# HGRN2 scores of 16 keys and fewer as 32 x 32 strips, sums with ones on four strips, mLSTM products on array halves

## The chip, the cores and the metric

The kernel runs on one core of one Trainium2 chip. A core has five engines with a queue of their own each: TensorE (PE, its weight loads are PEld), VectorE (DVE), ScalarE (ACT), GpSimd (POOL) and SyncE (SP), which here only starts DMAs. They share SBUF and PSUM, both of 128 partitions, and wait for each other through semaphores. The metric is the time of one execution in microseconds. Before the change it was 952.54 us, the median of three runs (952.47 to 953.07).

## What is computed

One decoder layer over 512 tokens of width 1024, in float32: a half-step SwiGLU feed-forward, a token mixer, and a second half-step feed-forward, each between RMS norms. The change is in the mixer, which projects the normalised tokens once and runs two recurrences on the columns, four heads of HGRN2 and four of mLSTM:

```python
def hgrn2(q, k, v, log_f):          # k = 1 - f, 4 heads, dk = dv = 128
    # S_t = diag(f_t) S_{t-1} + k_t v_t^T,  o_t = S_t^T q_t, by chunks:
    G = cumsum(log_f)
    o_inter = (q * exp(G)) @ S
    scores[t, s] = sum_d q[t, d] * k[s, d] * exp(G[t, d] - G[s, d])   # s <= t
    o = o_inter + scores @ v
    S = exp(G_end) * S + (k * exp(G_end - G)).T @ v

def mlstm(q, k, v, log_i, log_f):   # 4 heads, dqk = 64, dv = 128
    # m_t is the running maximum that keeps the exponents small
    P = (q @ k.T) * exp(D - m_t)
    num = inter * (q @ C) + P @ v;   den = inter * (q @ n) + sum(P)
    h = num / max(abs(den), exp(-m_t))
    C = keep * C + (w * k).T @ v;    n = keep * n + (w * k).sum()
```

Before mLSTM, its q and k columns go through a causal depthwise convolution of four taps with a bias, and SiLU. Both outputs are normalised, gated and projected back.

## The kernel before

Tokens stand in four chunks of 128 (`NT`), and both recurrences are worked by chunks of 128. The large matrix products are made of fp32r parts: every weight tile is split into a high and a low part (`split`: a cast on ScalarE, L208, a subtraction on VectorE, L210), and each product is three matmuls (`mm3`, L126 to L128, with 512 moving columns; `in_k`, L433, with 256). Small products are plain fp32: a matmul then appears in the trace as two instructions.

The mixer (`mixer`, L1371) runs a chain of small work on all engines, and fills TensorE's time between its steps with the projections. These stand in `self.jobs` as generators: `fill(n)` takes n steps of the next jobs, a step being three matmuls of 512 columns or six of 256; `until(name)` takes steps until a job is done. So the order on TensorE is written out by hand, as far as the program goes; a scheduler then orders each engine's queue by what is ready, keeping the dependences. `FILL` (L27) says how many steps are taken between two levels of head pair 0, of pair 1, between the mLSTM value stages and between the HGRN2 value stages.

HGRN2's scores with their decay inside the sum are made level by level for a pair of heads (`hgrn_levels`, L1065). At level c (64, 32, 16, 8, 4, 2) each block of 2c tokens has c keys and the c queries behind them; both are scaled by the decay to the block's middle (`hgrn_level`, L1032): VectorE makes two differences (L1044 for qe, L1045 for el), ScalarE their exponents (L1046, and L1047 into `ke`), VectorE multiplies by q (L1049). Then come eight chunk-and-head products (L1057). At 64 and 32, keys of the block stand as 64 or 32 stationary columns and write to the partitions of those keys. Below 32 all 128 keys of a chunk are multiplied with all 64 queries of that level, and VectorE picks the wanted entries by a mask (`put`, L1030, a copy with a predicate into `sT`, keys on partitions, 16 chunk-and-head blocks of 128 queries). At 64 and 32 ScalarE copies the block (L1027). Two `ke` tiles take turns.

The diagonal and the neighbours (level 1, `hgrn_lowest`, L984) are sums over the 128 features: VectorE makes "one" = q·k (L994) and "near" (L996, L997), both are split in high and low parts (ScalarE L995 and L998 into tiles that carry the tags of the norm gains, gpre and gpost; VectorE L1000, L1001), and TensorE multiplies them by a 128 x 128 matrix of ones (L1007), which puts the sum on all partitions; VectorE takes the diagonal by the mask `eye` (L1012). The tile "one" and the later "ek" (`hgrn_decays`, L969 and L970), whose transposes (L981) give the keys for the state, share one buffer of the tag xn.

The convolution (`conv`, L1188) copies the projection from PSUM (ScalarE, L1192) and makes four products on VectorE, the first with the bias (L1195), three added to it (L1198). In mLSTM, `mlstm_scores` makes the state products of three chunks for both head pairs (L1287): keys of two heads on 128 columns with the values of both heads, 258 columns, of which only the two diagonal blocks are kept. `mlstm_values` (L1324) multiplies the queries of a pair with the state C (L1332, 258 columns, zero off the diagonal blocks) and adds the scores times the values (L1335); then ScalarE squares, VectorE and GpSimd make the factor and VectorE scales.

`masks` (L883) makes ones, masks and eye on GpSimd. Scratch tiles of 512 columns come from a ring of four buffers (`st`), PSUM tiles from a ring of eight banks (`ps`).

Of the kernel before, what the change touches and what calls it, by code (L numbers as in the profile page):

```python
# [14 lines left out]
P = 128  # L15
# [11 lines left out]
FILL = (6, 5, 2, 2)  # L27
NH = 4
W = 512
# [38 lines left out]
class Layer:  # L68
# [814 lines left out]
    def masks(self, mc, mb):  # L883

        nc = self.nc

        self.ones = mb.tile([P, P], F32R, name="ones")
        nc.gpsimd.tensor_copy(self.ones, self.one.broadcast_to([P, P]))
        self.mask = mb.tile([P, len(LEVELS), 64], I32, name="mask")
        nc.gpsimd.memset(self.mask, 1)  # L890
        for n, c in enumerate(LEVELS):
            m = self.mask[:, n, :].rearrange("p (b c) -> p b c", c=c)
# [4 lines left out]
        self.eye = mb.tile([P, P], I32, name="eye")  # L897
        nc.gpsimd.memset(self.eye, 1)
        nc.gpsimd.affine_select(
            self.eye, self.eye, pattern=[[1, P]], compare_op=ALU.is_equal, fill=0.0, base=0, channel_multiplier=-1  # L900
        )

        sel = mb.tile([4, 6, 2, 64], F32, tag="tmp", bufs=1, name="sel")
        nc.gpsimd.memset(sel, 1.0)
# [79 lines left out]
    def hgrn_lowest(self, p):  # L984

        nc = self.nc
        q, kk = self.q[p], self.kk[p]
        flat = lambda t: t.rearrange("p a t -> p (a t)")
        by2 = lambda t: flat(t).rearrange("p (b two) -> p b two", two=2)
        by_a = lambda t: t.rearrange("p (a t) -> p a t", a=2)  # L990
        hi, lo = (by_a(self.cp.tile([P, D], F32R, tag=tag, bufs=1, name=self.nm(tag))) for tag in ("gpre", "gpost"))
# [3 lines left out]
        nc.scalar.copy(hi, one)  # L995
# [4 lines left out]
        nc.vector.tensor_tensor(lo, one, hi.bitcast(F32), op=ALU.subtract)  # L1000
        nc.vector.tensor_tensor(nlo, near, nhi.bitcast(F32), op=ALU.subtract)  # L1001
        yield
        scs = []
        for ops in ((hi[:, 0], lo[:, 0]), (hi[:, 1], lo[:, 1]), (nhi, nlo)):
            sc = self.ps()
            for n, m in enumerate(ops):
                nc.tensor.matmul(sc, self.ones, m, start=n == 0, stop=n == 1)  # L1007
            scs.append(sc)
        yield
        for a in range(2):  # L1010
            h = 2 * p + a
            nc.vector.copy_predicated(  # L1012
                self.sT[:, 4 * h : 4 * h + 4, :], self.eye[:, None, :].broadcast_to([P, NT, P]),
                scs[a].rearrange("p (n s) -> p n s", s=P),
            )
        self.put(p, 0, scs[2])
        yield

    def put(self, p, n, sc):

        c = LEVELS[n]
        so = self.sT[:, 8 * p : 8 * p + 8, :].rearrange("p n (b two c) -> p n b two c", two=2, c=c)[:, :, :, 1, :]
        if c >= 32:
# [5 lines left out]
        mk = self.mask[:, n : n + 1, :].broadcast_to([P, 8, 64]).rearrange("p n (b c) -> p n b c", c=c)  # L1029
        self.nc.vector.copy_predicated(so, mk, sc.rearrange("p (n b c) -> p n b c", n=8, c=c))  # L1030

    def hgrn_level(self, p, n, ke):  # L1032
# [19 lines left out]
        k8, q8 = flat(ke).rearrange("p (n s) -> p n s", s=P), qe.rearrange("p (n u) -> p n u", u=64)  # L1052
        for m in range(8):
            for b in range(1 if c < 32 else 64 // c):
                r = slice(2 * c * b, 2 * c * b + c) if c >= 32 else slice(0, P)
                u = slice(c * b, c * b + c) if c >= 32 else slice(0, 64)
                nc.tensor.matmul(  # L1057
                    sc[r, 64 * m + u.start : 64 * m + u.stop], k8[:, m, r], q8[:, m, u], start=True, stop=True,
                    skip_group_check=True,
                )  # L1060
# [4 lines left out]
    def hgrn_levels(self, p, kes, per, then=lambda: None):  # L1065
# [3 lines left out]
        next(L[0])  # L1069
# [19 lines left out]
        next(L[N - 1])  # L1089

# [97 lines left out]
    def conv(self, n, ps):  # L1188
# [6 lines left out]
        nc.vector.tensor_scalar(y, x, tap(3), self.prm[:, 16 + n : 17 + n], op0=ALU.mult, op1=ALU.add)  # L1195
# [33 lines left out]
    def mlstm_scores(self, mc):  # L1229
# [54 lines left out]
        for c in range(3):  # L1284
            for p in range(2):
                ps = self.ps()
                nc.tensor.matmul(  # L1287
                    ps[:, :258], self.kw[:, p, c, :], self.vm[:, c, 2 * p : 2 * p + 2, :].rearrange("p a v -> p (a v)"),
                    start=True, stop=True,
                )  # L1290
# [33 lines left out]
    def mlstm_values(self, c):  # L1324
# [3 lines left out]
        pm = []  # L1328
        for p in range(2):
            ps = self.ps()  # L1330
            if c:
                nc.tensor.matmul(ps[:, :258], self.qdm[:, p, (c - 1) * P : c * P], self.C[:, p, c - 1, :], start=True, stop=False)  # L1332
            for a in range(2):
                o = ps[:, 129 * a : 129 * a + 129]
                nc.tensor.matmul(o, self.pT[:, 2 * p + a, s], self.vm[:, c, 2 * p + a, :], start=c == 0, stop=c == 0 or a == 1)  # L1335
            pm.append(ps[:, :258].rearrange("p (a v) -> p a v", a=2))
        sq = self.sp.tile([P, 512], F32, tag="junk", bufs=1, name=self.nm("sq"))
        den, ab, ss, r = self.col(4), self.col(4), self.col(4), self.col(4)
        for p in range(2):
            nc.scalar.activation(sq[:, 256 * p : 256 * p + 256].rearrange("p (a v) -> p a v", a=2), pm[p][:, :, :P], AF.Square)  # L1340
        yield
        for p in range(2):
            nc.vector.tensor_copy(den[:, 2 * p : 2 * p + 2].rearrange("p (a o) -> p a o", o=1), pm[p][:, :, P : P + 1])
# [9 lines left out]
        for p in range(2):  # L1353
            nc.vector.tensor_tensor(
                self.y[:, c, W + 256 * p : W + 256 * p + 256].rearrange("p (a v) -> p a v", a=2),
                pm[p][:, :, :P],
                f[:, 2 * p : 2 * p + 2].rearrange("p (a o) -> p a o", o=1).broadcast_to([P, 2, P]),
# [195 lines left out]
```

## Time and profile before

| | us |
|---|---|
| median of three runs | 952.54 |
| the profiled execution | 953.22 |
| its span, first to last instruction | 951.5 |
| TensorE busy in it | 941.4 |
| VectorE busy | 714.3 |
| ScalarE busy | 466.1 |
| GpSimd busy | 291.2 |

The mixer with its projections lies between about 360 and 600 us of the span. In a row of the profile the first name is the source line and engine, then the operation, the tile written and the tiles read, the shape, and the count; a duration in the timeline is that of the whole group in that row, from the first start to the last end. Matmuls overlap each other, so what one costs is read from start to start, or from the chain of waits, which counts each stretch of time once.

### The profile page before, as it was taken

To read this page: it belongs to the slowest core of one execution; us is meant where nothing else is said; L and a number is where in the kernel's file an instruction comes from. 1 tells how busy PE (TensorE), PEld (TensorE's weight loads), DVE (VectorE), ACT (ScalarE), POOL (GpSimd) and SP (SyncE) were. 2 spreads that over 40 slices of the span, in tenths; PEclk is the share of its full clock that TensorE was granted. 3 is DMA by queue.
4 is the path that set the end of the run, shared out by engine and by line. 5 is a ranking of instruction groups with operands and counts; after the bars stand their busy time and mean duration, and the time that the engine had idled before them with its cause. 6 is when DMAs were issued, how large, how long until landed. Compare 5 with 4: busy or idle time off the path is not lost.

```text
span 951.5 us, 15926 instructions
## 1 busy us (share of the span) xinstructions
PE 941.4 (99%) x6567; PEld 865.2 (91%) x6567; DVE 714.3 (75%) x798; ACT 466.1 (49%) x632; POOL 291.2 (31%) x225
## 2 busy tenths in 40 slices
PE   9999999999999999999999999999999999999997
PEld 7999999999888889998788888999999999988885
DVE  6798999998445376799856555797999999843543
ACT  7645454445344356966523345763445444533431
POOL 3546555751000036200010300354655565100001
PEclk9999999999999999999999999999999999999999
DMA  9243333325322014321312126214334332322202
GB/s 319 81 134 113 110 120 124 113 91 175 110 90 89 1 36 121 90 90 49 129 45 72 42 87 196 90 48 128 102 105 129 116 112 89 109 96 105 89 1 88
DMA packets 81666, 95.97 MB, mean 101 GB/s; under 512 B 4117, under 2 KB 61497, under 8 KB 81594
## 3 DMA queue, kind: packets, MB, share of 16 engines
q1 hardware_dynamic: 81306, 94.44, 31.0%
q8 instruction: 51, 0.84, 0.4%
q10 hardware_dynamic: 288, 0.52, 0.2%
q14 instruction: 21, 0.17, 0.1%
HBM read 92.85 MB, written 2.10 MB: 100 GB/s over the span
## 4 chain that ended last, share of the span: by engine, by line
PE 96%; DVE 2%; issue 1%; ACT 1%; DMA 0%; POOL 0%; DVEq 0%; POOLq 0%; ACTq 0%
PE ps L488 45%; PE ps L126 12%; PE ps L128 12%; PE ps L127 12%; PE ps L433 6%; PE ps L1057 2%; PE ps L267 2%; PE ps L443 1%; PE ps L115 0%; PE ps L1130 0%; PE ps L1335 0%; PE ps L1308 0%; PE ps L1332 0%; PE ps L1097 0%; PE ps L1310 0%
## 5 line engine op out<-in xcount | busy, mean ns | idle before, releaser
L210 DVE TENSOR_TENSOR w<-raw,w 128x1024 fp32r<-128x1024 f32 x214 | 363.0, 1704 | 123.1 <-ACT w L208 122.9
L208 ACT CAST w<-raw 128x1024 fp32r<-128x1024 f32 x214 | 224.0, 1053 | 314.6 <-PE ps L128 114.2
L222 POOL TENSOR_TENSOR raw<-raw,raw 128x1024 f32<-128x1024 f32 x80 | 221.0, 2764 | 170.8 <-DVE w L210 160.3
L488 PE MATMUL ps<-xq,w 128*128 128x256 f32 x2016 | 238.1, 277 | 0.0
L488 PEld LDWEIGHTS ps<-xq,w 128*128 128x128 f32 x2016 | 233.7, 188 | 0.2
L488 PE MATMUL ps<-sq,w 128*128 128x256 f32 x1440 | 171.0, 277 | 0.0
L488 PEld LDWEIGHTS ps<-sq,w 128*128 128x128 f32 x1440 | 167.4, 188 | 0.0
L128 PE MATMUL ps<-w,hs 128*128 128x512 f32 x336 | 131.0, 390 | 0.0
L126 PE MATMUL ps<-w,hs 128*128 128x512 f32 x336 | 130.9, 390 | 0.0
L127 PE MATMUL ps<-w,hs 128*128 128x512 f32 x336 | 130.8, 389 | 0.0
L126 PE MATMUL ps<-w,xq 128*128 128x512 f32 x208 | 84.7, 407 | 0.1
L128 PE MATMUL ps<-w,xq 128*128 128x512 f32 x208 | 81.1, 391 | 0.0
L127 PE MATMUL ps<-w,xq 128*128 128x512 f32 x208 | 81.1, 390 | 0.0
L128 PEld LDWEIGHTS ps<-w,hs 128*128 128x128 f32 x336 | 63.1, 188 | 13.8 <-DVE hs L672 0.7
L127 PEld LDWEIGHTS ps<-w,hs 128*128 128x128 f32 x336 | 63.1, 188 | 12.9
L126 PEld LDWEIGHTS ps<-w,hs 128*128 128x128 f32 x336 | 63.1, 188 | 12.8
L354 POOL TENSOR_SCALAR col<-col 128x1 f32<-128x1 f32 x24 | 9.5, 397 | 203.2 <-ACT junk L353 203.1
L433 PE MATMUL ps<-xq,w 128*128 128x256 f32 x480 | 55.7, 277 | 0.0
L433 PEld LDWEIGHTS ps<-xq,w 128*128 128x128 f32 x480 | 55.1, 188 | 0.1
L672 DVE TENSOR_TENSOR hs<-hf,hs 128x1024 fp32r<-128x1024 f32 x42 | 51.1, 1218 | 0.0
L128 PEld LDWEIGHTS ps<-w,xq 128*128 128x128 f32 x208 | 39.1, 188 | 8.9 <-DVE xq L274 0.3
L126 PEld LDWEIGHTS ps<-w,xq 128*128 128x128 f32 x208 | 39.1, 188 | 8.7 <-ACT xq L273 0.7
(241 smaller groups left out, 963.4 us busy)
## 6 DMA issues: line engine op xcount, KB each, us to landing
raw<-in_ffn_w_in_dram SPq DMA_DIRECT2D x88, 512.0 KB, 4.1
raw<-in_ffn_w_out_dram SPq DMA_DIRECT2D x44, 512.0 KB, 3.4
raw<-in_w_mix_in_dram SPq DMA_DIRECT2D x28, 512.0 KB, 3.7
raw<-in_w_mix_out_dram SPq DMA_DIRECT2D x8, 512.0 KB, 3.5
out_dram<-xs SPq DMA_DIRECT2D x8, 256.0 KB, 2.0
xs<-in_x_dram SPq DMA_DIRECT2D x6, 256.0 KB, 6.8
gpost<-in_norm_post_dram SPq DMA_DIRECT2D x3, 512.0 KB
gpre<-in_norm_pre_dram SPq DMA_DIRECT2D x2, 512.0 KB, 4.1
```

The costliest lines, as they stand in the source:

```text
L126: mm(ps, sh, mh, start=start, stop=False, **kw)
L127: mm(ps, sh, ml, start=False, stop=False, **kw)
L128: mm(ps, sl, mh, start=False, stop=stop, **kw)
L208: nc.scalar.copy(hi, raw)
L210: nc.vector.tensor_tensor(lo, raw, hi.bitcast(F32), op=ALU.subtract)
L222: nc.gpsimd.tensor_tensor(o, o, c, op=ALU.add)
L267: self.nc.tensor.transpose(pt[:, c * P : (c + 1) * P], src[:, k * P : (k + 1) * P], self.ident)
L433: mm(ps[:, u0:u1], w[:, a, k, :], self.xop(k, b, u0, u1), start=k + n + m == 0, stop=k == ND - 1 and n == 2, skip_group_check=True,)
L443: self.nc.tensor.matmul(ps[:, :HALF], w[:, a, k, :], self.xop(k, b, 0, HALF), start=m + k == 0, stop=m == 2 and k == ND - 1)
L488: self.nc.tensor.matmul(ps[:, c], wb[b][:, k, v], left[d][:, k, :], start=first and a + n + k == 0, stop=n == 2 and k == KH - 1, skip_grou ...
L672: self.nc.vector.tensor_tensor(t[:, 1], src, t[:, 0].bitcast(F32), op=ALU.subtract)
L1057: nc.tensor.matmul(sc[r, 64 * m + u.start : 64 * m + u.stop], k8[:, m, r], q8[:, m, u], start=True, stop=True, skip_group_check=True,)
```

## The change

- The levels of 16, 8, 4 and 2 multiply each strip of 32 keys with the 16 queries that its own blocks have (four matmuls per chunk and head, writing to four groups of 32 partitions). VectorE's masked copies go into a new compact tile D (keys on partitions, 32 queries of the same strip); when all levels are made, `spread` copies D's four strips into sT on ScalarE.
- The level of 64 is made in two strips of 32 keys.
- The sums with ones take "one" and "near" as they are, in fp32, without splitting; each strip of 32 partitions sums its own 32 (or 16) columns only.
- mLSTM's state product is made per head on half the columns of the array, the query-times-state product per head on half its rows; the PSUM banks then hold one head of each pair instead of both heads of one pair.
- The first product of the convolution, with the bias, moves from VectorE to ScalarE.
- FILL[0] is 7 instead of 6. The masks are made wide in scratch tiles, and compacted by eight copies on GpSimd.

```diff
-FILL = (6, 5, 2, 2)
+FILL = (7, 5, 2, 2)
...
-        self.ones = mb.tile([P, P], F32R, name="ones")
-        nc.gpsimd.tensor_copy(self.ones, self.one.broadcast_to([P, P]))
-        self.mask = mb.tile([P, len(LEVELS), 64], I32, name="mask")
-        nc.gpsimd.memset(self.mask, 1)
+        self.ones = mb.tile([P, 32], F32, name="ones")
+        nc.gpsimd.memset(self.ones, 1.0)
+        self.D = mb.tile([P, 16, 32], F32, name="D")
+        nc.gpsimd.memset(self.D, 0.0)
...
+        self.mask = mb.tile([P, n16, 16], I32, name="mask")
+        self.eye = mb.tile([P, 32], I32, name="eye")
+        wide = self.st("wide", dt=I32)[:, : 64 * n16].rearrange("p (n c) -> p n c", n=n16)
+        square = self.st("square", P, dt=I32)
...
+        for b in range(4):
+            r = slice(32 * b, 32 * b + 32)
+            nc.gpsimd.tensor_copy(self.mask[r], wide[r, :, 16 * b : 16 * b + 16])
+            nc.gpsimd.tensor_copy(self.eye[r], square[r, r])
...
-        near, nhi, nlo = self.st("near"), self.st("nhi", dt=F32R), self.st("nlo", dt=F32R)
+        near = self.st("near")
         nc.vector.tensor_tensor(one, q, kk, op=ALU.mult)
-        nc.scalar.copy(hi, one)
...
-        nc.scalar.copy(nhi, near)
-        yield
-        nc.vector.tensor_tensor(lo, one, hi.bitcast(F32), op=ALU.subtract)
-        nc.vector.tensor_tensor(nlo, near, nhi.bitcast(F32), op=ALU.subtract)
-        yield
-        scs = []
-        for ops in ((hi[:, 0], lo[:, 0]), (hi[:, 1], lo[:, 1]), (nhi, nlo)):
-            sc = self.ps()
-            for n, m in enumerate(ops):
-                nc.tensor.matmul(sc, self.ones, m, start=n == 0, stop=n == 1)
-            scs.append(sc)
-        yield
-        for a in range(2):
-            h = 2 * p + a
-            nc.vector.copy_predicated(
-                self.sT[:, 4 * h : 4 * h + 4, :], self.eye[:, None, :].broadcast_to([P, NT, P]),
-                scs[a].rearrange("p (n s) -> p n s", s=P),
-            )
-        self.put(p, 0, scs[2])
+        yield
+        sc = self.ps()
+        for v, t, w in ((sc[:, :256], one.rearrange("p a (c t) -> p (a c) t", c=NT), 32), (sc[:, 256:384], near.rearrange("p (n t) -> p n t", n=8), 16)):
+            for b in range(4):
+                nc.tensor.matmul(
+                    v[32 * b : 32 * b + 32].rearrange("p (n t) -> p n t", n=8), self.ones, t[:, :, w * b : w * b + w],
+                    start=True, stop=True, skip_group_check=True,
+                )
+        yield
+        nc.vector.copy_predicated(
+            self.D[:, 8 * p : 8 * p + 8, :], self.eye[:, None, :].broadcast_to([P, 8, 32]), sc[:, :256].rearrange("p (n t) -> p n t", n=8)
+        )
+        self.put(p, 0, sc[:, 256:384])
...
-        if c >= 32:
+        if c > 16:
...
+        so = self.D[:, 8 * p : 8 * p + 8, :].rearrange("p n (b two c) -> p n b two c", two=2, c=c)[:, :, :, 1, :]
+        mk = self.mask[:, n : n + 1, :].broadcast_to([P, 8, 16]).rearrange("p n (b c) -> p n b c", c=c)
+        self.nc.vector.copy_predicated(so, mk, sc[:, :128].rearrange("p (n b c) -> p n b c", n=8, c=c))
+
+    def spread(self, p):
+
+        for b in range(4):
+            r = slice(32 * b, 32 * b + 32)
+            self.nc.scalar.copy(self.sT[r, 8 * p : 8 * p + 8, r], self.D[r, 8 * p : 8 * p + 8, :])
...
+        if c == 64:
+            blocks = [(slice(s, s + 32), slice(0, 64), 0) for s in (0, 32)]
+        elif c == 32:
+            blocks = [(slice(64 * b, 64 * b + 32), slice(32 * b, 32 * b + 32), 32 * b) for b in range(2)]
+        else:
+            blocks = [(slice(32 * b, 32 * b + 32), slice(16 * b, 16 * b + 16), 0) for b in range(4)]
         for m in range(8):
-            for b in range(1 if c < 32 else 64 // c):
...
+            for r, u, o in blocks:
+                o += m * (64 if c > 16 else 16)
+                nc.tensor.matmul(sc[r, o : o + u.stop - u.start], k8[:, m, r], q8[:, m, u], start=True, stop=True, skip_group_check=True)
...
         next(L[N - 1])
+        self.spread(p)
...
-        nc.vector.tensor_scalar(y, x, tap(3), self.prm[:, 16 + n : 17 + n], op0=ALU.mult, op1=ALU.add)
+        nc.scalar.activation(y, ps, AF.Identity, scale=tap(3), bias=self.prm[:, 16 + n : 17 + n])
...
-                nc.tensor.matmul(
-                    ps[:, :258], self.kw[:, p, c, :], self.vm[:, c, 2 * p : 2 * p + 2, :].rearrange("p a v -> p (a v)"),
-                    start=True, stop=True,
-                )
+                for a in range(2):
+                    r, v = slice(64 * a, 64 * a + 64), slice(129 * a, 129 * a + 129)
+                    nc.tensor.matmul(
+                        ps[r, v], self.kw[:, p, c, r], self.vm[:, c, 2 * p + a, :], start=True, stop=True, skip_group_check=True
+                    )
...
-            if c:
-                nc.tensor.matmul(ps[:, :258], self.qdm[:, p, (c - 1) * P : c * P], self.C[:, p, c - 1, :], start=True, stop=False)
...
+        banks = [self.ps() for _ in range(2)]
+        if c:
+            for p in range(2):
+                for a in range(2):
+                    r = slice(64 * a, 64 * a + 64)
+                    nc.tensor.matmul(
+                        banks[a][:, 129 * p : 129 * p + 129], self.qdm[r, p, (c - 1) * P : c * P],
+                        self.C[r, p, c - 1, 129 * a : 129 * a + 129], start=p == 0, stop=False, skip_group_check=True,
+                    )
+        for a in range(2):
+            for p in range(2):
+                o = banks[a][:, 129 * p : 129 * p + 129]
+                nc.tensor.matmul(
+                    o, self.pT[:, 2 * p + a, s], self.vm[:, c, 2 * p + a, :], start=c == 0, stop=True, skip_group_check=True
+                )
```

The lines of the changed kernel stand somewhat further down: its level matmuls are L1068, the transposes of ek L989, the state product L1297, query times state L1342, scores times values L1349; the sums keep L1007.

More of the change, by code (lines that the diff above doesn't have):

```diff
@@ L1021, in put @@
         c = LEVELS[n]
-        so = self.sT[:, 8 * p : 8 * p + 8, :].rearrange("p n (b two c) -> p n b two c", two=2, c=c)[:, :, :, 1, :]
-        if c >= 32:
+        if c > 16:
+            so = self.sT[:, 8 * p : 8 * p + 8, :].rearrange("p n (b two c) -> p n b two c", two=2, c=c)[:, :, :, 1, :]
             sc3 = sc.rearrange("p (n b c) -> p n b c", n=8, c=c)
@@ L1068, in hgrn_levels @@
         N = len(L)
-        next(L[0])
         next(L[0])
@@ L1327, in mlstm_values @@
         s = slice(c * P, (c + 1) * P)
-        pm = []
-        for p in range(2):
-            ps = self.ps()
-            if c:
[L1332 to L1336, printed above, removed]
+        banks = [self.ps() for _ in range(2)]
[13 more added lines that the diff above has]
+                )
+        pm = [ps[:, :258].rearrange("p (q v) -> p q v", q=2) for ps in banks]
+        of = lambda t, a: t.rearrange("p (q a v) -> p a q v", q=2, a=2)[:, a]
         sq = self.sp.tile([P, 512], F32, tag="junk", bufs=1, name=self.nm("sq"))
@@ L1354, in mlstm_values @@
             nc.vector.tensor_tensor(
-                self.y[:, c, W + 256 * p : W + 256 * p + 256].rearrange("p (a v) -> p a v", a=2),
+                of(self.y[:, c, W:], p),
                 pm[p][:, :, :P],
-                f[:, 2 * p : 2 * p + 2].rearrange("p (a o) -> p a o", o=1).broadcast_to([P, 2, P]),
+                of(f, p).broadcast_to([P, 2, P]),
                 op=ALU.mult,
```

23 lines of the change are left out of this document (7 added, 16 removed).

## The prediction

> **What bounds the kernel now.** I read the page first: its shares of busy time, then the chain that ended last.
>
> ```profile
> span 951.5 us, 15926 instructions
> PE 941.4 (99%) x6567; PEld 865.2 (91%) x6567; DVE 714.3 (75%) x798; ACT 466.1 (49%) x632; POOL 291.2 (31%) x225
> PE 96%; DVE 2%; issue 1%; ACT 1%; DMA 0%; POOL 0%; DVEq 0%; POOLq 0%; ACTq 0%
> ```
>
> TensorE is busy 99% of the span and makes 96% of the chain, so a change pays by what it takes from TensorE's own queue or from TensorE's waits; time taken from the other engines pays only where they make TensorE wait. So the second view was what TensorE waits for, and the third the busy times by stage of the mixer.
>
> ```profile
> PE ps L1057 <- ACT ke L1047: 1.5, 1, 1.5
> ```
> ```profile
> 398.00:440.00 42.00, 42.00 (x359) 40.00 (x358) 40.53 (x57) 30.76 (x42) 0.00 (x0) 1.00 0.23 73
> 440.00:460.00 20.00, 18.52 (x92) 15.20 (x92) 18.47 (x24) 12.31 (x16) 0.00 (x0) 1.00 0.33 109
> 460.00:490.00 30.00, 30.00 (x218) 26.11 (x216) 16.73 (x24) 11.84 (x20) 0.93 (x1) 1.00 0.29 86
> 490.00:545.00 55.00, 54.95 (x314) 45.55 (x313) 35.26 (x101) 20.79 (x37) 12.85 (x21) 1.00 0.15 49
> ```
>
> The columns are the stretch, its length, then busy time of PE, PEld, DVE, ACT and POOL, the granted clock, and the DMA. In the whole mixer TensorE stands still once, for 1.5 us before the level of 64 of head pair 1. VectorE is full (40.5 of 42 us) through pair 0 and (18.5 of 20) up to that wait. The clock is 1.00 throughout.
>
> **TensorE's part, term by term.** The chain at two levels of pair 1 shows what blocks of either kind cost (start, us, what):
>
> ```profile
> 465.92 0.63 PE ps L1057 x32
> 466.55 0.43 PE ps L126
> 466.98 0.23 PE ps L127
> ...
> 470.18 1.73 PE ps L1057 x16
> 471.91 0.29 PE ps L126
> ```
>
> The level of 32 already works on strips of 32 keys: 16 matmuls, two passes each, 32 instructions in 0.63 us, 19.7 ns each; the first filler matmul behind it takes 0.43 us against the usual 0.23, so leaving the strips costs 0.20. The level of 16, with all 128 keys as the stationary side, takes 1.73 us for 16 instructions (108 ns each) and 0.06 to leave, 1.79 together.
>
> *Levels of 16, 8, 4, 2* (eight blocks over two pairs): each becomes 32 matmuls of a 32-key strip and 16 queries, 64 instructions. No row shows 16 moving columns. The nearest row is the level of 32, with the same strip and twice the columns: 64 × 19.7 = 1.26, plus 0.20 to leave, 1.46 in place of 1.79, a gain of 0.33 a block and 2.6 in all. If the four strips run side by side where the level of 32 uses two, an instruction costs half, the block 0.83, the gain is 7.7. The other bound is the rival below.
>
> By the Trainium skill, "TensorEngine Tiling (Array Packing)", Key Properties, a change of tiling mode drains the engine; the 0.20 us behind the strips agrees. By "TensorE: Matmul & The Clock Gate", "Wait — 56ns, not 53.3ns?", starts never come closer than about 25 ns however few columns there are; the 19.7 ns here are below that, and the row decides. An estimate by that page would be 64 × 25 = 1.6 us a block, and no gain from the levels.
>
> *Level of 64* (two blocks): now 16 instructions with 64 stationary columns, ending where the transposes begin:
>
> ```profile
> 410.74 1.15 PE L1057 MATMUL ps<-qe,ke 128*64 128x64 f32 x16
> 411.82 0.87 PE L981 MATMUL ps<-ident,ek 128*128 128x128 f32 x6
> ```
>
> 1.08 us from start to start, 67.5 ns each. After: two strips of 32, 32 instructions, 64 moving columns. Bounds 32 × 19.7 = 0.63, and 1.08 if the columns that stream set the time as now and two strips halve it. I take 0.98, nearer the latter since the columns stay: gain 0.2 for both pairs (0 to 0.9). The level of 32 keeps its instructions.
>
> *Sums with ones* (twice): now six fp32r matmuls of 512 columns, in one pass each; after, sixteen instructions in fp32, since every matmul takes two passes: 8 of 256 columns and 8 of 128 on four strips, 3072 columns.
>
> ```profile
> 399.04 0.40 PE L1007 MATMUL ps<-gpre,ones 128*128 128x512 f32 x1
> 400.44 0.63 PE L433 MATMUL ps<-xq,w 128*128 128x256 f32 x4
> ```
> ```profile
> 499.96 1.16 PE L1223 MATMUL ps<-qk 64*128 64x128 f32 x16
> 500.88 0.48 PE L1185 MATMUL ps<-nm,selr 36*128 36x512 f32 x1
> ```
> ```profile
> 527.95 0.60 PE L1332 MATMUL ps<-C,qdm 128*128 128x258 f32 x2
> 528.38 0.61 PE L1335 MATMUL ps<-vm,pT 128*128 128x129 f32 x4
> ```
>
> Now: 400.44 − 399.04 = 1.40. The fp32 column costs 0.43/(2 × 258) = 0.83 ns on the whole array (L1332) and 0.92/(16 × 128) = 0.45 ns where matmuls alternate between two halves (L1223). Four strips in order b = 0 to 3, both passes of one strip following each other, can overlap neighbours as the halves do: 3072 × 0.45 = 1.38, plus 0.20 to leave, 1.58: a loss of 0.18 each, 0.4 together. Bounds: no overlap 2.56 + 0.20, a loss of 2.7 for both; all four at once 0.64 + 0.20, a gain of 1.1. I take the halves, whose order is the same. The bound by strips that never overlap is far from the level of 32, where they do.
>
> *mLSTM states and values.* The state product of a chunk is four instructions of 258 columns now:
>
> ```profile
> 512.31 1.03 PE L1287 MATMUL ps<-vm,kw 128*128 128x258 f32 x4
> 513.00 0.58 PE L126 MATMUL ps<-w,xq 128*128 128x512 f32 x1
> 513.41 0.39 PE L127 MATMUL ps<-w,xq 128*128 128x512 f32 x1
> ```
>
> From start to the second filler 1.10, less one filler of 0.23: 0.87. After: eight of 129 columns on alternating halves, 8 × 129 × 0.45 = 0.46 and 0.20 to leave, 0.66; gain 0.2, three chunks. The query-times-state product (L1332, four of 258 columns over both pairs, 0.86) becomes the same eight on row halves, in three chunks: 0.2 each again. Together 1.2 (bounds: no overlap, 0.86 + 0.20, a loss of 1.2; no cost of leaving, a gain of 2.5). The products with pT keep count and shape.
>
> Sum on TensorE: 2.6 + 0.2 − 0.4 + 1.2 = 3.6.
>
> **The wait of 1.5 us.** It is VectorE's queue, not ScalarE's: just ahead of ke stands el.
>
> ```profile
> 458.43 0.61 DVE el L1045
> ...
> 459.06 0.64 ACT ke L1047
> ...
> 459.78 1.12 PE ps L1057 x16
> ```
> ```profile
> L1030 DVE COPY_PREDICATED sT<-mask,ps 128x512 f32<-128x512 int32 x6 | 6.1, 1021 | 0.1
> L1012 DVE COPY_PREDICATED sT<-eye,ps 128x512 f32<-128x512 int32 x4 | 2.7, 736 | 0.0
> L969 DVE TENSOR_TENSOR ek<-G,kk 128x1024 f32<-128x1024 f32 x2 | 2.5, 1226 | 0.1
> L1000 DVE TENSOR_TENSOR gpost<-one,gpre 128x1024 fp32r<-128x1024 f32 x2 | 2.4, 1223 | 0.8 <-ACT gpre L995 0.8
> L1195 DVE TENSOR_SCALAR qk<-cx,prm 128x512 f32<-128x512 f32 x4 | 2.1, 534 | 0.0
> L1001 DVE TENSOR_TENSOR nlo<-near,nhi 128x512 fp32r<-128x512 f32 x2 | 1.4, 688 | 0.1
> ```
>
> The change takes from VectorE both subtractions (1.2 + 0.7 a pair) and the four conv products (2.1), lets one eye copy of 256 columns replace two of 512, and cuts each masked copy from 512 to 128 columns; at a quarter of its 1.0 us a masked copy keeps some 0.3, an estimate. Between 440 and 459 us alone that is a subtraction, two masked and two eye copies: about 0.7 + 1.5 + 1.1 = 3.3 us, more than the 1.5. In the built program VectorE also makes the level-64 operands of pair 1 ahead of the copies of the sums, and FILL[0] of 7 puts seven more steps of filler (three matmuls of 0.23) before them: 4.8 us more cover. The wait goes: 1.5. What is late next is nothing I can find: for the levels of pair 1 five steps and a block are 5 × 0.69 + 1.46 = 4.9 us each, and VectorE is busy 16.7 of 30 us there even now.
>
> **Costed at nothing.** The seven steps are taken from later filler: the built program still has an unbroken run of filler ahead of the turn of y; without it they would bare the latencies of the value stages. ScalarE loses two casts a pair and gains four conv products and eight copies of D to sT:
>
> ```profile
> L1027 ACT COPY sT<-ps 32x256 f32<-32x256 f32 (+1 forms) x6 | 2.6, 433 | 0.0
> L1409 ACT ACTIVATE q<-ps 128x512 f32<-128x512 f32 x4 | 2.4, 600 | 0.0
> ```
>
> 8 × 0.43 + 4 × 0.60 = 5.9 us, spread over stretches where it is idle 11 of 42, 8 of 20 and 18 of 30 us; sT is read only after mLSTM. A new wait: ek (L969) shares its buffer with "one", which the sums now read, so ek stands behind TensorE's sums, and behind ek in VectorE's queue the sums' copies and the next el. TensorE has 36 fillers (8.3 us) between the sums of pair 1 and the transposes of ek; ek takes 1.2 there and about 1.1 on ScalarE as exponent; without that cover it would cost 2.3. GpSimd makes more masks and copies, which nothing reads before the sums at 399, and then it idles for long:
>
> ```profile
> 386.62 0.73 POOL L904 MEMSET sel<- 4x768 f32 x1 [11.99 <-DVE G L946]
> ```
>
> On SP's queue the loads of gpost and gpre move up (their tiles no longer serve the sums), between the weight loads at 350 to 362 us.
>
> ```profile
> 354.24 0.70 DVE L390 TENSOR_TENSOR ps<-ps,gpost 128x512 f32<-128x512 f32 x1
> 349.81 9.10 SPq L183 DMA_DIRECT2D raw<-in_w_mix_in_dram  x4
> ```
>
> The gpost load waits for the last reader of the old gain, done at 354.9, and the weight load behind it is the third of those four, whose own buffer comes free later; no delay. A late weight would cost its lateness.
>
> **The sum.** 3.6 + 1.5 = 5.1. The profiled execution took 953.22 us (span 951.5 and 1.7 around it), 0.7 above the median of 952.54. So 948.1 on its scale, 947.4 on the median's.
>
> **Rivals.**
> 1. *The issue of small instructions sets the time (slower).* The eight blocks carry 512 instructions. The transposes of 4 × 4 start 60 ns apart:
>
> ```profile
> 461.72 0.20 PE L1174 MATMUL ps<-ident,z 4*128 4x4 f32 x1
> 461.78 0.20 PE L1173 MATMUL ps<-ident,z 4*128 4x4 f32 x1
> ```
>
> At that price the levels lose 512 × 40 = 20.6 us: 968. It decides from 19.7 + 5.1/0.512 = 29.7 ns on. Against it: the level of 32 issues at 19.7, and those transposes all sit on the same array rows.
> 2. *A floor near 25 ns.* At (1.79 − 0.20)/64 = 24.8 ns a block gains nothing: 947.4 + 2.6 = 950.0. This is the case of the rule that the Trainium skill, "TensorE: Matmul & The Clock Gate", gives above.
> 3. *Strips and halves don't overlap in the longer matmuls.* Sums lose 2.7, mLSTM 1.2, the level of 64 gains nothing: 2.6 − 2.7 − 1.2 + 1.5 = 0.2, so 952.3: nothing measurable. For it: passes of one strip follow each other; against it: L1223.
> 4. *Four strips side by side.* Levels 7.7, sums 1.1: with the rest 7.7 + 0.2 + 1.1 + 1.2 + 1.5 = 11.7, so 940.8.
>
> **How the numbers follow.** Forecast 0.56, rival 1 0.11, rival 2 0.12, rival 3 0.11, rival 4 0.10. About 0.2% (1.9 us) is what a measurement here can tell from no change. Faster: 0.56 + 0.10 + most of rival 2, 0.08, is 0.74; same 0.11 + 0.04 = 0.15; slower 0.11. The range holds forecast, rivals 2 and 3 and the nearer half of 4: 942.5 to 952.5; the forecast's own is 944.5 to 950.
>
> **What would show it.** The L1068 blocks of 64 instructions at 1.2 to 1.3 us with 0.4 for the filler behind; L1007 of sixteen instructions at 1.4 to 1.6; L1297 and L1342 at about 0.46 a chunk; no wait of TensorE in the levels; VectorE below 36 of 42 us in pair 0. Wrong if an L1068 block takes over 1.6, or if TensorE waits for ke, ek or a weight.

## The result

The changed kernel takes 943.58 us (median of five runs, 943.38 to 943.65); the kernel before took 952.85 on the same chip (five runs, 952.47 to 953.55). The ratio is 0.9902, 95% interval 0.9889 to 0.9916: 9.3 us are gone where 5.1 were forecast. The measured time lies 3.8 us below the forecast of 947.4: inside the whole range (942.5 to 952.5), outside the forecast's own (944.5 to 950), and a good half of the way towards the rival with four strips side by side (940.8).

The page of the changed kernel, its span, busy times and the chain's shares:

```profile
span 941.9 us, 16851 instructions
...
PE 933.0 (99%) x7027; PEld 851.7 (90%) x7027; DVE 701.1 (74%) x788; ACT 470.0 (50%) x641; POOL 291.1 (31%) x234
...
PE 92%; DVE 3%; POOL 2%; issue 1%; ACT 1%; DVEq 0%; POOLq 0%; ACTq 0%
```

TensorE is busy 8.4 us less, with 460 matmul records more. The chain has passed from TensorE to the others in two places, and 5% of it now lies on VectorE and GpSimd: ahead of the mixer (343 to 360 us), and in the mixer's value stages (513 to 552 us). The waits of TensorE in the mixer after the change (total, times, longest), and three stretches with the columns that the prediction names:

```profile
PE ps L128 <- DVE xq L274: 0.3, 1, 0.3
PE ps L126 <- DVE y L1371: 0.3, 1, 0.3
PE ps L267 <- DVE hf L372: 0.2, 1, 0.2
```
```profile
398.00:440.00 42.00, 42.00 (x541) 38.29 (x540) 36.32 (x51) 35.71 (x48) 0.00 (x0) 1.00 0.29 87
440.00:460.00 20.00, 20.00 (x190) 15.72 (x189) 16.34 (x24) 12.77 (x21) 0.00 (x0) 1.00 0.22 62
...
482.00:537.00 55.00, 54.69 (x334) 43.15 (x334) 36.35 (x102) 20.07 (x37) 10.99 (x19) 1.00 0.18 58
```

The wait of 1.5 us before the level of 64 is gone; three of 0.2 to 0.3 have come, on hf at 360 us, on y at 524 and on xq at 552. VectorE is down to 36.3 of 42 us through pair 0, still a little over the 36 that were forecast. The chain of the changed kernel at the places of the change (start, us, what), and a level of 16 queries or fewer in its timeline:

```profile
411.92 1.02 PE ps L1068 x32
...
418.53 0.63 PE ps L1068 x32
...
436.54 0.67 PE ps L1068 x51
437.21 0.43 PE ps L126
437.64 0.23 PE ps L127
...
449.28 0.79 PE ps L1007 x16
450.06 0.43 PE ps L126
```
```profile
436.47 0.74 PE L1068 MATMUL ps<-qe,ke 128*32 128x16 f32 x64
```

A level of 16 queries takes 0.67 us where 1.73 stood and 1.26 was forecast (the chain counts 51 of the block's 64 instructions; the timeline has all of them). That is 0.67/64, 10.5 ns an instruction. Leaving costs 0.43 − 0.23 = 0.20, as forecast, so a block costs 0.87 in place of 1.79. The sixteen instructions of the sums take 0.79, and 0.20 to leave, where 1.40 stood and 1.58 was forecast. The level of 64 takes 1.02, where 1.08 stood, and the level of 32 (the row of 0.63) is as it was.

To compare kernels without what lies outside the mixer, I take the stretch from the first sums with ones to the first turn of y, in the timeline of the changed kernel and of the one before:

```profile
398.86 0.64 PE L1007 MATMUL ps<-one,ones 128*32 128x256 f32 x8
...
549.56 1.91 PE L267 MATMUL ps<-ident,y 128*128 128x128 f32 x16
```
```profile
559.20 1.91 PE L267 MATMUL ps<-ident,y 128*128 128x128 f32 x16
```

Before: 559.20 − 399.04 = 160.16 us (the first sum stands in the prediction). After: 549.56 − 398.86 = 150.70. The stretch gives 9.46 us, about as much as the whole kernel gives (9.3 by the medians, 951.5 − 941.9 = 9.6 by the spans of these two profiled executions), so the explanation is to be found in it. In each experiment below it is taken from the same two rows.

### The profile page after: what moved, and what is told of

Same layout as the page of the kernel before. It is cut to its first block, busy times and chain, and to the rows that moved or that the text cites. A ratio compares the mean times of both kernels' runs of the same rounds, so it can differ in the third digit from the quotient of the medians.

```text
span 941.9 us, 16851 instructions
## 1 busy us (share of the span) xinstructions
PE 933.0 (99%) x7027; PEld 851.7 (90%) x7027; DVE 701.1 (74%) x788; ACT 470.0 (50%) x641; POOL 291.1 (31%) x234
## 4 chain that ended last, share of the span: by engine, by line
PE 92%; DVE 3%; POOL 2%; issue 1%; ACT 1%; DVEq 0%; POOLq 0%; ACTq 0%
PE ps L488 46%; PE ps L126 12%; PE ps L128 12%; PE ps L127 12%; PE ps L433 6%; PE ps L267 1%; PE ps L1068 1%; POOL col L259 1%; POOL col L354 0%; DVE w L216 0%; PE ps L1138 0%; PE ps L115 0%; PE ps L122 0%; DVE y L1330 0%; ACT junk L353 0%
## 5 line engine op out<-in xcount | busy, mean ns | idle before, releaser
L126 PEld LDWEIGHTS ps<-w,xq 128*128 128x128 f32 x208 | 39.1, 188 | 10.2 <-issue 1.6
```

The source lines that it names most:

```text
L126: mm(ps, sh, mh, start=start, stop=False, **kw)
```

## The experiments

Of the theories, the first says that matmuls on different strips of 32 columns run side by side, and those on the same strip behind one another, so that the order over strips sets the time of a block. The rivals are that each instruction has a price of its own, whatever the order, or that the gain came from elsewhere (VectorE's relief, the filler, mLSTM). Each diff is against the changed kernel unless it says otherwise.

### The order over the strips

The same 64 instructions of a level block, in another order: all eight chunk-and-head blocks of one strip before the next strip, or two strips in turn and then the other two.

```diff
-        for m in range(8):
-            for r, u, o in blocks:
+            seq = [(m, blk_) for blk_ in blocks for m in range(8)]
...
+            for m, (r, u, o) in seq:
```
```diff
...
+            seq = [(m, blk_) for two in (blocks[:2], blocks[2:]) for m in range(8) for blk_ in two]
...
```

> The changed kernel, but in the levels of 16 to 2 the eight matmuls of one strip follow each other before the next strip's (same 64 instructions a block, other order). Strips side by side (a matmul overlaps its neighbour only on another strip): the block rises from 0.67 us to about four times, 64 x 42 ns = 2.7 us, eight blocks +16 us, about 960 us. Issue of small instructions alone (10.5 ns each, whatever the strip): block 0.67 us, 943.6 us.

> The changed kernel, with the strips of the levels of 16 to 2 taken in alternating pairs (strips 0 and 1 for all eight chunks and heads, then 2 and 3). Strips side by side: two overlap, as in the level of 32, 19.7 ns an instruction, block 1.26 us, +0.6 us x 8 = +4.7 us, about 948.3 us. Issue alone: block 0.67 us, 943.6 us.

Strip by strip the kernel took 952.82 us (one run), with a stretch of 159.86; two strips in turn 945.77 (945.71 to 946.61; ratio to before 0.9928, 0.9913 to 0.9943), stretch 153.39. The chain of the two, strip by strip first:

```profile
438.90 1.83 PE ps L1072 x64
440.73 0.43 PE ps L126
```
```profile
442.80 1.03 PE ps L1072 x62
443.82 0.43 PE ps L126
```

The block takes 1.83, 1.03 and 0.67 us with one, two and four strips in turn: 28.6, 16.1 and 10.5 ns an instruction. The exit costs 0.20 each time. Nothing but the order differs, so a price per instruction alone can't be the cause. Both orders cost time, as strips side by side would have it, and both less than was expected (952.82 against 960, 945.77 against 948.3): one strip in a row costs 2.7 times the four in turn, and not four times. Eight blocks of 1.83 − 0.67 make 9.3 us, and the stretch is 9.2 longer than that of the changed kernel, so the gain is gone: 952.82 us stand against 952.89 for the kernel before in the same set. With pairs it is 8 × 0.36 = 2.9 by the blocks and 2.7 by the stretch.

### Four strips at the levels of 64 and 32 too

These two levels stayed on two strips. Here every second chunk-and-head block of them writes to the two strips that lay idle, and ScalarE copies the result in two halves.

```diff
-                self.nc.scalar.copy(so[r, :, b], sc3[r, :, b])
+                for h in range(2):
+                    self.nc.scalar.copy(so[r, h::2, b], sc3[slice(r.start + c * h, r.stop + c * h), h::2, b])
...
+                ro = slice(r.start + c * (m % 2), r.stop + c * (m % 2)) if c > 16 else r
-                nc.tensor.matmul(sc[r, o : ...
+                nc.tensor.matmul(sc[ro, o : ...
```

> The changed kernel, with the levels of 64 and 32 on all four strips too: every second chunk and head writes to the partitions that the level leaves unused (64 to 127, or 32 to 63 and 96 to 127), and ScalarE copies the block in two halves. Strips side by side: level of 64 from 1.02 to 0.5 or 0.6 us, level of 32 from 0.63 to 0.35 us, twice each: -1.4 us, about 942.2 us, if the doubled ScalarE copies stay hidden. Issue alone, or columns that stream one after the other: no change, 943.6 us.

It took 942.05 us (941.53 to 942.46; ratio 0.9887, 0.987 to 0.9903), stretch 149.26. Its chain at the levels of 64 and 32:

```profile
411.79 0.58 PE ps L1070 x32
412.37 0.81 PE ps L989 x6
...
417.96 0.39 PE ps L1070 x32
```

1.02 became 0.58, and 0.63 became 0.39: 2 × (0.44 + 0.24) = 1.4 us by the blocks, 1.44 by the stretch. So the rotation pays with 64 and 32 moving columns too, at 18.1 and 12.2 ns an instruction. The whole times' intervals overlap (0.9902 and 0.9887); the blocks and the stretch show the difference, the runs alone don't.

### Half the columns

At the levels of 16 and fewer each strip is multiplied with half of its queries; the kernel leaves out the other half of these scores.

```diff
...
+                if c <= 16:
+                    u = slice(u.start, u.start + 8)
...
```

> Leaves out half of the scores: at levels 16, 8, 4 and 2 each strip of 32 keys is multiplied with the first 8 of its 16 queries only, and only those are copied; the number of instructions and the rotation over four strips stay. With 64 columns an instruction took 18.1 ns in rotation (level 64 with four strips), with 32 columns 12.2 ns, with 16 columns 10.5 ns. If the columns set the time, 8 columns take about half of 10.5 ns, a block 0.34 us in place of 0.67, and the kernel 8 x 0.33 = 2.7 us less: 940.9. If there is a floor near 10 ns an instruction (issue, or the weight load of a strip), the block stays at 0.65 and the time at 943.5 within 0.4.

It took 943.1 us (943.0 to 943.76), stretch 150.52. The chain:

```profile
436.85 0.65 PE ps L1074 x55
437.50 0.43 PE ps L126
```

Half the columns saved 0.02 us of 0.67. With four strips in turn an instruction takes 18.1, 12.2, 10.5 and 10.2 ns for 64, 32, 16 and 8 columns: it comes to rest near 10 ns, and the levels of 16 queries stand at that floor. Whether it is the issue or the weight load that sets it wasn't told apart.

### The sums in runs

The sums gained where a loss was forecast. Here they are cut finer, and the pieces of one strip follow each other before the next strip; the columns in all stay.

```diff
-        for v, t, w in ((sc[:, :256], ...
-            for b in range(4):
-                nc.tensor.matmul(
-                    v[32 * b : 32 * b + 32].rearrange("p (n t) -> p n t", n=8), self.ones, t[:, :, w * b : w * b + w],
...
+        for b in range(4):
+            for g in range(4):
+                for v, t, w in sums:
+                    nc.tensor.matmul(
+                        v[32 * b : 32 * b + 32].rearrange("p (n t) -> p n t", n=8)[:, 2 * g : 2 * g + 2], self.ones,
+                        t[:, 2 * g : 2 * g + 2, w * b : w * b + w],
```

> The sums with ones cut into matmuls of two blocks (64 and 32 columns, the same 3072 columns in all, 64 instructions a pair of heads in place of 16), the eight of one strip one behind the other before the next strip. If matmuls of one strip follow each other and only neighbours on other strips overlap, nearly all is serial: 3072 x 0.83 = 2.55 us in place of 0.79, twice, so 943.5 + 3.5 = 947.0 us. If TensorE takes instructions of other strips from far behind, or if the four strips pay however they are ordered, the sums stay near 0.8 to 1.0 us (64 x 12 to 18 ns) and the time within 0.4 us of 943.5.

It took 946.45 us (946.19 to 947.54; ratio 0.9936, 0.9921 to 0.9951), stretch 154.03. The chain:

```profile
398.50 2.47 PE ps L1009 x64
```

2.47 us in place of 0.79 for the same 3072 columns: 0.80 ns a column, as on the whole array, against 0.26 when the strips change after the two passes of one matmul. So two passes on one strip in a row still leave the neighbours room to run beside, sixteen in a row don't. Two sums make 2 × 1.68 = 3.4, the stretch gives 3.3. The finer cut has a part in it, which no run took alone: with four strips in turn, 32 instructions of 64 columns and 32 of 32 would take 32 × (18.1 + 12.2) = 0.97 us, an estimate from the rows of the levels above. By it some 1.5 of the 1.68 us are the order's.

### Two levels side by side

What entering and leaving the strips costs was read from a filler matmul that came late. Here the products of two levels of a unit are made one behind the other, with the filler of both behind them, so that six entries and exits fall away (`hgrn_edges` moves behind one level more with them); once alone, and once with four strips at 64 and 32.

```diff
-        for n in range(1, N):
+        for n in range(1, N, 2):
...
-            next(L[n])
...
-            self.fill(per)
+            for k in (n, n + 1):
+                next(L[k])
...
+            self.fill(2 * per)
```

> The changed kernel with the products of two levels of a unit taken one right behind the other (64 with 32, 16 with 8, 4 with 2), with the filler of both behind them: per pair of levels one entry and one exit of the strips less. If entering and leaving cost what the trace of the changed kernel shows (about 0.2 us behind the last strip and 0.08 us ahead of the first), six exits fewer bring 6 x 0.28 = 1.7 us: 941.9 us and a stretch from the sums to the first turn of y near 149.0 us. If the 0.43 us of the first filler matmul behind a block is only the ordinary tail of any change of shape, nothing comes: 943.5. If VectorE's operands of the second level of a pair now come late, TensorE waits ahead of levels 32, 8 and 2, and the time rises by that wait: above 944.5, with rows of waits on the gathered operands.

> Levels 64 and 32 too with four strips in turn (942.05 us alone), and the levels taken two at a time. If entries and exits cost 0.28 us each time, 942.05 - 1.7 = 940.4 us; if they are no cost, 942.0; if operands come late, above 942.6 with TensorE waiting ahead of the second level of a pair.

Alone it took 941.43 us (941.09 to 941.8; ratio 0.9882, 0.9866 to 0.9899), stretch 148.99; with four strips 940.68 (940.32 to 941.19; ratio 0.9874, 0.9859 to 0.9888), stretch 147.89. The chain of the first at a pair of levels:

```profile
440.25 1.25 PE ps L1068 x97
441.50 0.43 PE ps L126
441.93 0.24 PE ps L127
```

Two blocks take 1.25 us and one exit, 1.25 + 0.20 = 1.45 in place of 2 × 0.87 = 1.74. The stretch is 1.71 shorter than that of the changed kernel, 0.285 for each entry and exit saved: the price read from the one filler holds (0.20 behind, and 0.08 of start ahead of the block). With four strips 1.37 of the 1.7 came. The operands of the second level come in time; TensorE's waits are those of the changed kernel less the one on hf. The version with both is the fastest of all here, 2.9 us below the changed kernel, with intervals that just part (0.9888 against 0.9889).

### The wait of 1.5 us

Two causes were at hand: less work on VectorE, and the filler of seven steps in place of six. First the changed kernel with six, then the kernel before with seven.

```diff
-FILL = (7, 5, 2, 2)
+FILL = (6, 5, 2, 2)
```
```diff
-FILL = (6, 5, 2, 2)
+FILL = (7, 5, 2, 2)
```

> The changed kernel with FILL[0] back at 6. If VectorE's smaller load removed the wait before the level of 64 of pair 1: no such wait, 943.6 us. If the seven moved steps of filler removed it: the wait of up to 1.5 us is back, 945.1 us.

> The kernel before with FILL[0] at 7 and nothing else. If VectorE's queue makes the wait whatever the filler: it stays at 1 us or more, 952.8 us. If 4.8 us more filler cover it: it is gone, 951.3 us.

The changed kernel with six took 943.51 us (943.23 to 943.86), stretch 150.95, with no wait before the level of 64. TensorE waits once in its mixer:

```profile
PE ps L1342 <- DVE y L1371: 0.5, 1, 0.5
```

The kernel before with seven took 951.91 (951.12 to 952.18) against 953.06 for the kernel before in the same set; ratio 0.9988, 0.9979 to 0.9997; stretch 158.83. Its busy times up to that level, in the view by stretches, and TensorE's waits in its mixer:

```profile
398.00:440.00 42.00, 42.00 (x354) 39.76 (x354) 39.13 (x54) 31.61 (x43) 0.00 (x0) 1.00 0.25 67
440.00:460.00 20.00, 20.00 (x97) 16.71 (x97) 19.63 (x26) 11.90 (x17) 0.00 (x0) 1.00 0.38 118
```
```profile
PE ps L128 <- DVE xq L274: 0.3, 1, 0.3
PE ps L126 <- DVE y L1354: 0.2, 1, 0.2
```

TensorE is busy for all 20 us of the second row, where it had 18.52 before, though VectorE is as full as ever (19.63 of 20). So either cause alone takes the wait away, and one number in a constant would have had 1.3 of the 9.5 us. In the changed kernel the seven steps are worth nothing that these runs can tell. They have a price, too: the wait on xq, right behind the turn of y, stands in the trace of every kernel here with seven steps (0.28 to 0.45 us), that of the kernel before with seven among them, and in neither kernel with six. So the filler taken from the value stages is missed there.

### mLSTM on whole arrays, the convolution on VectorE

First mLSTM's products go back to the whole array, then the first product of the convolution to VectorE; the rest of the change stays.

```diff
+                nc.tensor.matmul(
+                    ps[:, :258], self.kw[:, p, c, :], self.vm[:, c, 2 * p : 2 * p + 2, :].rearrange("p a v -> p (a v)"),
+                    start=True, stop=True,
+                )
...
+            if c:
+                nc.tensor.matmul(ps[:, :258], self.qdm[:, p, (c - 1) * P : c * P], self.C[:, p, c - 1, :], start=True, stop=False)
```
```diff
-        nc.scalar.activation(y, ps, AF.Identity, scale=tap(3), bias=self.prm[:, 16 + n : 17 + n])
+        nc.vector.tensor_scalar(y, x, tap(3), self.prm[:, 16 + n : 17 + n], op0=ALU.mult, op1=ALU.add)
```

> The changed kernel with the mLSTM products on the whole array as before (state product 258 columns, query times state 258 columns). By the prediction's term the halves gain 0.2 us in each of six products: without them 944.8 us. By the trace of the changed kernel the halves gain about 0.1 us each and give back a wait of 0.3: without them 943.9 us. A rival in which the halves cost more than they save: 943.0 us.

> The changed kernel with the convolution's first product back on VectorE (four instructions of 0.53 us). Time taken from VectorE pays only where TensorE waits for it: no wait, 943.6 us. Rival: VectorE is full again in pair 0 and TensorE waits, up to +2.1 us, 945.7 us.

With whole arrays the time was 943.49 us (943.05 to 943.76), stretch 150.91, 0.2 longer than that of the changed kernel. With the convolution on VectorE it was 943.33 (942.97 to 943.68), stretch 150.57. Neither part is worth anything that the runs can tell. Why mLSTM's is not, three views show: the timeline of the changed kernel, that of the one with whole arrays, and the chain of the kernel before at the query products and values of one chunk:

```profile
506.54 0.39 PE L128 MATMUL ps<-w,xq 128*128 128x512 f32 x1
506.85 0.66 PE L1297 MATMUL ps<-vm,kw 128*64 128x129 f32 x8
507.45 0.50 PE L126 MATMUL ps<-w,xq 128*128 128x512 f32 x1
507.78 0.39 PE L127 MATMUL ps<-w,xq 128*128 128x512 f32 x1
...
515.35 0.40 PE L128 MATMUL ps<-w,xq 128*128 128x512 f32 x1
515.68 0.72 PE L1342 MATMUL ps<-C,qdm 64*128 64x129 f32 x8
516.32 1.16 PE L1349 MATMUL ps<-vm,pT 128*128 128x129 f32 x8
517.24 0.48 PE L126 MATMUL ps<-w,xq 128*128 128x512 f32 x1
517.55 0.39 PE L127 MATMUL ps<-w,xq 128*128 128x512 f32 x1
...
524.06 0.47 PE L126 MATMUL ps<-w,xq 128*128 128x512 f32 x1 [0.31 <-DVE y L1371]
...
552.27 0.50 PE L128 MATMUL ps<-w,xq 128*128 128x512 f32 x1 [0.34 <-DVE xq L274]
```
```profile
506.58 0.39 PE L128 MATMUL ps<-w,xq 128*128 128x512 f32 x1
506.81 1.03 PE L1295 MATMUL ps<-vm,kw 128*128 128x258 f32 x4
507.49 0.58 PE L126 MATMUL ps<-w,xq 128*128 128x512 f32 x1
507.91 0.39 PE L127 MATMUL ps<-w,xq 128*128 128x512 f32 x1
...
524.31 0.47 PE L126 MATMUL ps<-w,xq 128*128 128x512 f32 x1 [0.24 <-DVE y L1362]
```
```profile
521.52 0.43 PE ps L1332 x2
521.95 0.45 PE ps L1335 x4
522.40 0.44 PE ps L1332 x2
522.83 0.45 PE ps L1335 x4
```

Between the same two fillers the state product fills 507.78 − 506.54 = 1.24 us on halves and 507.91 − 506.58 = 1.33 on the whole array: 0.09 saved, where 0.2 was forecast. By starts, and less a filler of 0.23 ahead and behind, the whole array takes 0.68 + 0.19 = 0.87, the halves 0.08 to enter, 0.60 for the product (1032 columns, 0.58 ns each) and 0.10 to leave, 0.78. The query products with the values behind them take 517.55 − 515.35 − 2 × 0.23 = 1.74, against 0.43 + 0.45 + 0.44 + 0.45 = 1.77 before: next to nothing. The rows with a wait in brackets hold the new wait on y of the mLSTM values, 0.31 us, and 0.24 with whole arrays; behind it in the changed kernel stands the wait on xq, 0.34.

### The new wait on y

One more step of filler between the mLSTM value stages (the third number of the list), on top of the version with four strips at 64 and 32:

```diff
-FILL = (7, 5, 2, 2)
+FILL = (7, 5, 3, 2)
```

> Levels 64 and 32 with four strips in turn, and one more filler unit in the shares of the levels (7, 5, 3, 2), as they were, so that fewer are left for the mLSTM stage or more, and the wait of 0.3 us on y of the mLSTM values moves. If that wait of 0.3 us is the end of the path there and moves with the filler, the time falls by 0.3 us to about 941.7; if the stage is bound by its own chain of values, the time stays at 942.0 within 0.3.

It took 941.99 us (941.25 to 944.65) against 942.05, stretch 149.10 against 149.26. The wait on y is gone from the list of TensorE's waits, and 0.16 us of the stretch with it: half of it at most, and nothing in the whole time. The wait on xq behind it rose from 0.40 to 0.45, and from 511 to 550 us the chain still runs on VectorE and GpSimd. So the wait on y wasn't what ended the path there; by the chain it is the value stages' own work.

## Why the prediction was right, and where it was not

| term | forecast | measured | from |
|---|---|---|---|
| levels 16, 8, 4, 2 | 2.6 | 7.4 | 8 × (1.79 − 0.87) |
| level of 64 | 0.2 | 0.1 | 2 × (1.08 − 1.02) |
| sums with ones | −0.4 | 0.8 | 2 × (1.40 − 0.99) |
| mLSTM | 1.2 | 0.2 | the kernel with whole arrays |
| wait before level 64 | 1.5 | 1.3 to 1.5 | the kernel before with seven steps; its row before |
| new wait on y | 0 | −0.2 to −0.3 | the wait's rows, 0.24 and 0.31 |
| sum | 5.1 | 9.5 to 9.8 | the stretch gives 9.46 |

**The direction and the cause were right:** TensorE's own queue became shorter, and the wait went. Of what was costed at nothing, most came to nothing: no wait for a weight, for ek or for sT, and ScalarE took its 5 us more in pair 0 (35.7 of 42 us, 30.8 before) without a loss. One item came up: "The seven steps are taken from later filler: the built program still has an unbroken run of filler ahead of the turn of y". Up to that turn TensorE waits only on y, but the wait on xq behind it (0.34 us) comes with the seven steps, and the chain runs through the value stages' latencies.

**That the time fell inside the range was in part luck.** Levels and sums together gave what the fourth rival said but for 0.6 us, and the range ended 1.7 us short of that rival. The time came inside because mLSTM gave 1.0 us less than was forecast, the kernel before ran 0.3 longer, and new waits came.

**The levels were mis-sized.** The step that failed is "The nearest row is the level of 32, with the same strip and twice the columns: 64 × 19.7 = 1.26". It carried over the price of an instruction with two strips in turn to a loop that goes over four. The sentence behind it, "an instruction costs half, the block 0.83", is what the chip did: 10.5 ns, 0.87 with the exit. It was held as a bound with a chance of 0.10, though the new loop has four strips for each m where that of the level of 32 has two, and the prediction itself took that row as a sign that different strips overlap. The order experiments settle it: 28.6, 16.1 and 10.5 ns for one, two and four.

**The sums had the wrong sign.** The step: "Four strips in order b = 0 to 3, both passes of one strip following each other, can overlap neighbours as the halves do: 3072 × 0.45 = 1.38". The bound named behind it, "all four at once 0.64 + 0.20", is near what came: 0.79 + 0.20. Two passes in a row on a strip don't keep the other strips from running beside; the run of sixteen does.

**mLSTM was too dear.** The step: "8 × 129 × 0.45 = 0.46 and 0.20 to leave, 0.66; gain 0.2". Measured are 0.60 for the product and some 0.18 for entry and exit (1.24 − 2 × 0.23 − 0.60), 0.78. A column cost 0.58 ns where 0.45 had been read from a block of halves twice as long, and the entry was left out. That reading may have been too low already: it ends at the start of the product behind the block, while the chain of the kernel before counts 1.09 us for the block, 0.53 ns a column:

```profile
500.04 1.09 PE ps L1223 x16
```

"What is late next is nothing I can find" missed the wait on y, a small one; the kernel before with seven steps has it too (0.2 us), so it comes without the halves too.

**The wait** was rightly put to VectorE's queue, and the change does relieve it; but the seven steps of filler, given as further cover, would have been enough alone.

**Of the rivals,** the issue of small instructions at 60 ns and the floor near 25 ns fell with the row of 10.5 ns. By the Trainium skill, "TensorE: Matmul & The Clock Gate", "Wait — 56ns, not 53.3ns?", starts never come closer than about 25 ns; in this kernel that is near the truth for one strip in a row (28.6 ns), and wrong by more than a factor of two for four in turn. The third, no overlap in the longer matmuls, was right in its result for mLSTM and wrong for the sums. The fourth was right for levels and sums and came out 2.8 us too low: 1.0 of that is mLSTM, 0.7 lies in the levels and the sums (7.7 against 7.4, 1.1 against 0.8, 0.2 against 0.1), 0.3 is the new wait, and 0.3 the kernel before, which ran at 952.85 here and not at 952.54; the remaining 0.5 isn't put down to a term.

**What stays open:** what sets the floor of 10 ns with four strips, and the 28.6 ns of one strip in a row, more than twice the 16 × 0.83 = 13 ns of its columns at the price of the whole array. The sum of the terms, 9.5 to 9.8, is read from single traces and goes with the 9.46 of the stretch; 1.3 for the wait is already less a wait on y of 0.2, which the kernel before with seven steps has too. That the medians give 9.3 and the profiled executions 9.6 (953.22 against 943.60) comes from the profiled execution of the kernel before, 0.4 above its median. The waits on hf and xq lie outside the stretch, and are none of its terms.

## What to carry to other kernels

Read the price of a small matmul together with its neighbours in the queue: before a row's nanoseconds are carried over, count the strips that its loop has in turn and those of the new loop. Put the loop over strips innermost, and give a block all four strips even if each then has fewer columns; but each visit to the strips costs about 0.28 us at its two ends, so put such blocks side by side, and leave a product of under a microsecond on the whole array if halves save less than that. Where a wait goes, try the cheapest of its cures alone before the rewrite gets the credit.

## What the runs showed of the hardware

- The same 64 instructions of 32 stationary and 16 moving columns, fp32 in two passes, take 28.6, 16.1 or 10.5 ns each with one, two or four column strips in turn. By the Trainium skill, "TensorEngine Tiling (Array Packing)", "Theoretical Speedup", four tiles of 32 give up to four times; here they give 28.6 / 10.5 = 2.7 with 16 columns. The sums give 2.47 / 0.79 = 3.1, part of which is the finer cut (by the estimate of 0.97 us it would be 2.5).
- With four in turn the time comes to rest: 18.1, 12.2, 10.5, 10.2 ns for 64, 32, 16 and 8 columns.
- Entering and leaving the strips cost 0.285 us together (1.71 us for six), and are paid again at each change between strips and the whole array, not at each level.
